# Five adaLN modulations moved to TensorE as 256-column products with the condition stationary

## The chip, the cores and the metric

The kernel runs on one core of a Trainium2 chip. The metric is the device time of one execution in microseconds. The core has five engines with instruction queues of their own: PE (TensorE, with its weight loads shown apart as PEld), DVE (VectorE), ACT (ScalarE), POOL (GpSimd) and SP (SyncE, which here only issues transfers). PE's clock has two levels, 2.4 GHz (1.00 in the profile) and 1.2 GHz (0.50).

## The reference, cut to what matters

Two layers of a hybrid backbone over 128 context and 512 latent tokens, 1024 wide, all in float32. Each layer first makes six modulation vectors from a condition, one set for the context tokens and one for the latent ones:

```
mod = silu(cond) @ w_ada[l] + b_ada[l]          # (1024) @ (1024, 6144), for cond = c_ctx and c
shift1, scale1, gate1, shift2, scale2, gate2 = split(mod, 6)
h = rmsnorm(x, norm1_g) * (1 + scale1) + shift1
x = x + gate1 * mixing(h)                        # latent attention, differential attention, SSD scan, one projection
h = rmsnorm(x, norm2_g) * (1 + scale2) + shift2
x = x + gate2 * (relu(h @ w_ff1)**2 @ w_ff2)
```

Below, a modulation is named (l, j): layer l, and j from 0 to 5 in the order above. One modulation is 1024 x 1024 weights, 4 MB, times two condition vectors.

## The kernel before, in words

Activations lie with features on the 128 partitions and the 640 tokens along the row. Each layer has a mixing part (`mixing`, L571) and a feed-forward part (`feed_forward`, L1845). Large products are done as three products of float32 values split into a high and a low part. The mixing part has five stages: the convolution inputs and values; the remaining projections woven with the SSD scan (`ps_proj`, `ps_ssd`); the scan's tail, woven with the start of differential attention (attention B); attention B with the first part of the output projection (`woc`); latent attention (attention A) with a second part of the output projection. A tail adds the last part of the projection (`wo2`), the residual and the squares and scales for norm2 (`nrm2.scaled`, `nrm2.square`).

The modulations are made as fill work between these. Each is needed late: gate1 (j = 2) where the output projection first adds to x (L539), and shift2 and scale2 (j = 3, 4) where norm2 scales x (L493, L494). There are three ways in which one is made:

- `AdaPE` (L355): at the very start, (0, 1) and (0, 0). Not touched by the change.
- `ada_pe(l, j)` (L439): TensorE with the weights stationary. For each 128 output columns, eight products of a 128 x 128 block of w_ada with the two condition columns (L456), accumulated in one PSUM bank, then a small copy by ACT (L457). A full float32 product stands in the profile as two records, so a step of eight products is 16. Before the change it makes (0, 2) and (0, 3), in 16 steps.
- `ada_rows(items)` (L397): DVE with transposed weights. First PE spreads each condition vector over all partitions (`crow`, L406). Then DVE multiplies each 128 x 512 piece of weights with it and sums along the row (output `junk`, L427). A modulation is 32 such instructions. Before the change it makes (0, 4) in the mixing part of layer 0, (1, 3) and (1, 4) in that of layer 1, and five more in the feed-forward parts, which the change leaves alone.

`ada_first` chains the first layer's three. `gates_made` tells when gate1 of layer 0 is there: after the scan's tail the kernel steps the fill until it is.

The order of the work is written as generators. `weave` (L186) always steps the part with the smallest (k + 0.5) / n, where k counts its steps and n is its pace. The fill's pace is set three times per mixing part by `FILL[l]`: for the projections, for the scan's tail together with attention B, and for attention A; `pace(n)` sets k back to 0. What is left runs behind attention A. The framework places instructions on the engines in an order that starts from this one, and an instruction waits for what it reads and for a free buffer of its kind. Buffers are of a few kinds: G (48 of them, 642 columns), X (6, 648 columns), Y (13, 512 columns), and PSUM banks (PB: 3). All weights and all x tiles are fetched by SP in one queue (wr by L266 and L1745, x by L239).

Of the kernel before, what the change touches and what calls it, by code (L numbers as in the profile page):

```python
# [21 lines left out]
P = 128  # L22
D = 1024
KD = D // P
# [72 lines left out]
SLOT = 576  # L97
GW = T + 2

ADA_T = [(0, 4), (0, 5)] + [(1, j) for j in (1, 0, 2, 3, 4, 5)]  # L100
NG, NX, NXS = 48, 6, 13
NWR, NWH, NWL = 7, 6, 5

# [1 line left out]
def build(nc, tc, a, ctx):  # L105
    vec, act, pool, pe = nc.vector, nc.scalar, nc.gpsimd, nc.tensor
# [7 lines left out]
    def mark(s):  # L114
        if MARK:
            MARK(nc, s)
# [15 lines left out]
    def nm(s):  # L132
        uid[0] += 1
        return f"{s}_{uid[0]}"

    def size(shape):
        n = 1
        for s in shape[1:]:
            n *= s
        return n  # L140
# [11 lines left out]
    def Y(shape, dt=F32, name="t"):  # L152

        assert size(shape) <= 512, shape
        return sp.tile(list(shape), dt, tag="Y", name=nm(name), bufs=NXS)

    def S(shape, tag, bufs=2, dt=F32):
        return sp.tile(list(shape), dt, tag=tag, name=nm(tag), bufs=bufs)
# [4 lines left out]
    def PB(name="pb"):  # L163
        return psp.tile([P, 512], F32, tag="pb", name=nm(name), bufs=3)
# [4 lines left out]
    def f(ap):  # L169
        return ap.bitcast(F32)  # L170
# [52 lines left out]
    ident, ones = f(identr), f(masksr[:, 4])  # L223
# [4 lines left out]
    sc = cp.tile([P, KD, 2], F32, name="sc")  # L228
# [17 lines left out]
    def V(l, name, i=0, n=1):  # L246
        o = VEC[name][0] + i
        return vecs[:, l, o:o + n]
# [56 lines left out]
    def evac_split(hi, lo, src):  # L305
        act.copy(out=hi, in_=src)
        vec.tensor_tensor(out=lo, in0=src, in1=f(hi), op=ALU.subtract)  # L307
# [27 lines left out]
    def ada_finish(l, j, ps, ms=slice(0, KD)):  # L335

        n = ms.stop - ms.start
        b = V(l, "bada", j * 8 + ms.start, n)
        vec.tensor_tensor(out=mods[l][:, j, ms], in0=ps, in1=b.unsqueeze(2).to_broadcast([P, n, 2]), op=ALU.add)
        if j in (1, 4):  # L340
            g = V(l, "g1" if j == 1 else "g2", ms.start, n)
            vec.scalar_tensor_tensor(out=amul[l][:, j // 4, ms], in0=mods[l][:, j, ms], scalar=1.0,
                                     in1=g.unsqueeze(2).to_broadcast([P, n, 2]), op0=ALU.add, op1=ALU.mult)
        if j in (0, 3):
            evac_split(shh[l][:, j // 3, ms], shl[l][:, j // 3, ms], mods[l][:, j, ms])
# [51 lines left out]
    def ada_rows(items):  # L397

        mark("fill")
        row = [[Y([P, 512], name="crow") for _ in range(2)] for _ in range(2)]  # L400
        for v in range(2):
            for h in range(2):
                pt = PB("crow")
                for i in range(4):
                    k = 4 * h + i
                    pe.matmul(pt[:, i * P:(i + 1) * P], sc[:, k, v:v + 1].to_broadcast([P, P]), ident, start=True, stop=True)  # L406
                act.copy(out=row[v][h], in_=pt)
        units = [(l, j, m, h) for l, j in items for m in range(KD) for h in range(2)]

        def fetch(i):  # L410
            l, j, m, h = units[i]
            raw = Y([P, 512], name="wa")
            nc.sync.dma_start(raw, a["w_adaT"][ADA_T.index((l, j)), m, :, h * 512:(h + 1) * 512])
            return raw

        raws = [fetch(0), fetch(1)]
        for i, (l, j, m, h) in enumerate(units):
            if m == 0 and h == 0:
                res = S([P, 2, KD, 2], "adares", 2)
            for v in range(2):  # L420
                junk = X([P, 512], name="junk")
                sum_ = res[:, h, m, v:v + 1]
                if 2 * h + v in ROWS_POOL:
                    pool.tensor_tensor(out=junk, in0=raws[i], in1=row[v][h], op=ALU.mult)
                    act.activation(out=junk, in_=junk, func=AF.Copy, accum_out=sum_)
                else:
                    vec.scalar_tensor_tensor(out=junk, in0=raws[i], scalar=1.0, in1=row[v][h], op0=ALU.mult, op1=ALU.mult,  # L427
                                             accum_out=sum_)
            if i + 2 < len(units):
                raws.append(fetch(i + 2))  # L430
            if h == 1:
                if m == KD - 1:
                    sm = S([P, 8, 2], "adapt", 2)
                    vec.tensor_tensor(out=sm, in0=res[:, 0], in1=res[:, 1], op=ALU.add)
                    ada_finish(l, j, sm)
                yield
                mark("fill")

    def ada_pe(l, j):  # L439

        def fetch(m):
            raw = [Y([P, 4, P], name="wa") for _ in range(2)]
            for h in range(2):
                c = j * 1024 + m * P
                nc.sync.dma_start(raw[h], a["w_ada"][h * 512:(h + 1) * 512, c:c + P].rearrange("(k p) c -> p k c", p=P))
            return raw

        raws = [fetch(0)]
        res = S([P, KD, 2], "adapt", 2)
        for m in range(KD):  # L450
            mark("fill")
            if m + 1 < KD:
                raws.append(fetch(m + 1))
            ps = PB("adap")
            for k in range(KD):
                pe.matmul(ps[:, 0:2], raws[m][k // 4][:, k % 4], sc[:, k], start=(k == 0), stop=(k == KD - 1))  # L456
            act.copy(out=res[:, m], in_=ps[:, 0:2])  # L457
            if m == KD - 1:
                ada_finish(l, j, res)
            yield  # L460

    gates_made = []

    def ada_first():

        for m, _ in enumerate(ada_pe(0, 2)):
            if m == KD - 1:
                gates_made.append(0)
            yield
        yield from ada_pe(0, 3)  # L470
        yield from ada_rows([(0, 4)])

# [96 lines left out]
    def mixing(l, nrm, fill, late=None, raws={}):  # L571
# [1074 lines left out]

        fills = FILL[l]
        pace(fills[0])
# [45 lines left out]
    AHEAD = 1  # L1694
    FETCHED, AHEADS = 7, 2
    AP1, AP0 = (1, 4), ()
    FILL = (2, 20, 9), (8, .01, 9)
    ROWS_POOL = ()
    CONV_POOL = ()
    ON_POOL = {f"xbc{j}" for j in range(2, 6)} | {"dv0", "dv1"}  # L1700
# [299 lines left out]
        act.copy(out=masksr[:, 0:4, :], in_=mk)  # L2000
        act.activation(out=never, in_=mk[:, M_SF:M_SB + 1], func=AF.Copy, scale=-1e30)
    for l in range(DEPTH):
        f0 = Part(ada_first() if l == 0 else ada_rows([(1, 3), (1, 4)]), 1)
        n2 = mixing(l, nrm, f0, *((second, raws0) if l == 0 else ()))
        f1 = Part(ada_rows([(0, 5), (1, 1), (1, 0), (1, 2)] if l == 0 else [(1, 5)]), 57)
        nrm = feed_forward(l, n2, f1)
# [64 lines left out]
def host_inputs(i):  # L2071
    c_ = np.ascontiguousarray
    fm = lambda v: v.reshape(DEPTH, -1, P).transpose(0, 2, 1)
    arr = {}
    x = np.concatenate([i["x_prompt"][0], i["x_sample"][0]], axis=0)
    arr["xT"] = c_(x.reshape(T, KD, P).transpose(2, 1, 0))
    cc = np.stack([i["c_ctx"], i["c"][0]], axis=0)
    arr["cT"] = c_(cc.reshape(2, KD, P).transpose(2, 1, 0))
    ad = i["w_ada"].reshape(DEPTH, D, 6, KD, P)
    arr["w_ada"] = c_(i["w_ada"][0, :, :5 * D])  # L2080
    arr["w_adaT"] = c_(np.stack([ad[l, :, j].transpose(1, 2, 0) for l, j in ADA_T]))
    arr["W"] = _pack(i["w_in"], i["w_uq"], i["w_ukv"], i["w_out"], i["w_ff1"], i["w_ff2"])
    cw = i["ssm_conv_w"].reshape(DEPTH, CONV_K, 6, P).transpose(0, 3, 2, 1).reshape(DEPTH, P, 30)
    gsub = np.concatenate([i["diff_subln_g"]] * 2, axis=1)[:, :, None]
    arr["vecs"] = c_(np.concatenate([fm(i["norm1_g"]), fm(i["norm2_g"]), fm(i["b_ada"]), fm(i["mla_q_norm_g"]),
                                     fm(i["mla_kv_norm_g"]), cw, fm(i["ssm_conv_b"]), gsub, fm(i["ssm_norm_g"])], axis=2))
    row = np.concatenate([i["mla_qk_norm_q"], i["mla_qk_norm_k"], i["diff_q_norm_g"], i["diff_k_norm_g"],
                          i["diff_lq1"], i["diff_lk1"], i["diff_lq2"], i["diff_lk2"],
                          i["ssm_A_log"].reshape(DEPTH, 16), i["ssm_dt_bias"].reshape(DEPTH, 16), i["ssm_D"]], axis=1)
    arr["rows"] = c_(np.broadcast_to(row[:, None, :], (DEPTH, P, NROW)))  # L2090
    arr["cdk"] = c_(i["cache_diff_k"][0].reshape(DEPTH, P, 256))
    arr["cdv"] = c_(i["cache_diff_v"][0].reshape(DEPTH, P, 256))
    arr["ckr"] = c_(i["cache_mla_krope"][0])
    arr["cckvT"] = c_(i["cache_mla_ckv"][0].transpose(0, 2, 1))
    st = i["state_ssm"][0].reshape(DEPTH, 2, 2, 4, P_C, N_C)
    arr["h0"] = c_(st.transpose(0, 2, 5, 1, 3, 4).reshape(DEPTH, P, 512))
    arr.update(_shape_consts())
    return arr
# [31 lines left out]
```

## Time and profile before

| | us |
|---|---|
| three runs: median (lowest to highest) | 1838.31 (1832.51 to 1839.88) |
| the profiled execution | 1843.01 |
| its span, first to last instruction | 1841.2 |
| mean granted clock of PE | 0.948 |
| busy: PE, PEld, DVE, ACT, POOL | 1752.6, 1659.3, 1330.3, 828.8, 464.5 |

The profiled execution is one run with the profiler on; its span leaves out 1.8 us around the instructions. Busy time is the union of an engine's instructions. Matmuls are pipelined, so a record lasts longer than the step from its start to the start of the next; the step is what it costs PE in a run of such records.

### The profile page before, as it was taken

The page shows a single profiled execution, that of the slowest core. Times are in us where ns is not written, and L with a number is a line of the kernel's source. Part 1 is how long each engine was busy: PE and PEld are TensorE (multiplying, and loading weights), DVE is VectorE, ACT ScalarE, POOL GpSimd, SP SyncE. Part 2 cuts the span into 40 slices and gives each one's busy share as a digit, 9 for nine tenths or more (in the row PEclk, how much of TensorE's full clock was granted, in tenths as well). Part 3 has the DMA queues.
Part 4 walks back from the last instruction along what each step waited for, and adds up shares of the span by engine and source line. Part 5 has one row for each costly group of instructions (what it writes and reads, how often), then busy time and mean ns, then how long its engine had stood idle before and what let it go on. Part 6 is the DMA issues. An engine that isn't in the chain of part 4 may idle for free. (4 is left out here: it accounts for less than half of the span.)

```text
span 1841.2 us, 31851 instructions
## 1 busy us (share of the span) xinstructions
PE 1752.6 (95%) x11764; PEld 1659.3 (90%) x11764; DVE 1330.3 (72%) x2788; ACT 828.8 (45%) x1737; POOL 464.5 (25%) x538
## 2 busy tenths in 40 slices
PE   6999999999989999999997999889999999999999
PEld 4798778998989999999997987779999999999998
DVE  6774867568578988685776778989677877475562
ACT  7553327554445452432544443387534445243340
POOL 1433433101120231404135244431003032130400
PEclk8899866899999999999999999889999999999999
DMA  9122113344143437264441232202424242525341
GB/s 336 56 78 71 52 35 88 103 136 146 32 136 117 138 100 260 93 213 154 149 159 48 76 107 68 69 25 84 138 88 127 86 131 81 186 87 161 112 157 56
DMA packets 122732, 209.02 MB, mean 114 GB/s; under 512 B 13392, under 2 KB 32720, under 8 KB 122576
## 3 DMA queue, kind: packets, MB, share of 16 engines
q1 hardware_dynamic: 122016, 206.80, 35.2%
q8 instruction: 93, 1.52, 0.3%
q14 instruction: 63, 0.52, 0.1%
q10 hardware_dynamic: 560, 0.18, 0.0%
HBM read 179.51 MB, written 27.43 MB: 112 GB/s over the span
## 5 line engine op out<-in xcount | busy, mean ns | idle before, releaser
L1775 ACT CAST wh<-wr 128x512 fp32r<-128x512 f32 x232 | 143.9, 621 | 316.0 <-PE fm L1805 205.2
L1805 PE MATMUL fm<-ul,wh 128*128 128x320 f32 x1024 | 235.0, 311 | 10.2 <-DVE ul L307 10.2
L1776 DVE TENSOR_TENSOR wl<-wr,wh 128x512 fp32r<-128x512 f32 x232 | 179.0, 780 | 79.8 <-issue 44.6
L1805 PE MATMUL fm<-uh,wh 128*128 128x320 f32 x1024 | 234.8, 310 | 0.1
L1805 PE MATMUL fm<-uh,wl 128*128 128x320 f32 x1024 | 234.5, 310 | 0.0
L1762 POOL TENSOR_TENSOR wS<-wr,wr 128x512 f32<-128x512 f32 x48 | 78.7, 1639 | 495.2 <-DMA wr<-in_W 213.9
L1805 PEld LDWEIGHTS fm<-ul,wh 128*128 128x128 f32 x1024 | 172.3, 189 | 11.3 <-DVE ul L307 11.3
L427 DVE SCALAR_TENSOR_TENSOR junk<-wa,crow 128x512 f32<-128x512 f32 x256 | 176.7, 739 | 7.4 <-DMA wa<-in_w_adaT 5.7
L1805 PEld LDWEIGHTS fm<-uh,wh 128*128 128x128 f32 x1024 | 172.4, 189 | 0.5 <-issue 0.3
L1805 PEld LDWEIGHTS fm<-uh,wl 128*128 128x128 f32 x1024 | 172.3, 189 | 0.0
L539 DVE SCALAR_TENSOR_TENSOR x<-fm,mod,x 128x128 f32<-128x128 f32 (+2 forms) x192 | 72.5, 432 | 107.7 <-PE fm L1805 104.7
L759 PE MATMUL tm<-wl,hhi 128*128 128x256 f32 (+2 forms) x400 | 120.0, 300 | 5.7 <-POOL wl L297 4.0
L1775 ACT CAST wh<-wS 128x512 fp32r<-128x512 f32 x96 | 59.8, 622 | 141.7 <-PE fm L1805 70.5
L758 PE MATMUL tm<-wh,hhi 128*128 128x256 f32 (+2 forms) x400 | 120.0, 300 | 3.0 <-DVE zth L779 2.4
L760 PE MATMUL tm<-wh,hlo 128*128 128x256 f32 (+2 forms) x400 | 119.2, 298 | 0.0
L296 ACT CAST wh<-wr 128x512 fp32r<-128x512 f32 (+2 forms) x108 | 66.8, 625 | 75.6 <-PE fm L318 34.6
L1805 PE MATMUL ffx<-eh,wh 128*128 128x320 f32 x288 | 89.4, 311 | 0.0
L1805 PE MATMUL ffx<-eh,wl 128*128 128x320 f32 x288 | 88.9, 309 | 0.0
L1805 PE MATMUL ffx<-el,wh 128*128 128x320 f32 x288 | 88.9, 309 | 0.0
L759 PEld LDWEIGHTS tm<-wl,hhi 128*128 128x128 f32 x400 | 80.2, 200 | 8.0 <-POOL wl L297 4.2
L539 DVE SCALAR_TENSOR_TENSOR x<-wo,mod,x 128x128 f32<-128x128 f32 (+1 forms) x144 | 57.0, 432 | 39.0 <-PE wo L318 38.5
L758 PEld LDWEIGHTS tm<-wh,hhi 128*128 128x128 f32 x400 | 80.1, 200 | 5.1 <-DVE zth L779 2.8
(386 smaller groups left out, 4837.1 us busy)
## 6 DMA issues: line engine op xcount, KB each, us to landing
wr<-in_W SPq DMA_DIRECT2D x351, 256.0 KB, 2.8
wa<-in_w_adaT SPq DMA_DIRECT2D x128, 256.0 KB, 4.5
xsave<-x SPq DMA_DIRECT2D x72, 320.0 KB, 2.2
x<-xsave SPq DMA_DIRECT2D x72, 320.0 KB, 4.0
war<-in_w_ada SPq DMA_DIRECT2D x32, 256.0 KB, 5.3
wa<-in_w_ada SPq DMA_DIRECT2D x32, 256.0 KB, 3.4
x<-in_xT SPq DMA_DIRECT2D x16, 320.0 KB, 5.5
out_yT<-x SPq DMA_DIRECT2D x8, 320.0 KB, 2.2
```

The costliest lines, as they stand in the source:

```text
L296: act.copy(out=hi[:, :w], in_=raw[:, :w])
L427: vec.scalar_tensor_tensor(out=junk, in0=raws[i], scalar=1.0, in1=row[v][h], op0=ALU.mult, op1=ALU.mult, accum_out=sum_)
L539: vec.scalar_tensor_tensor(out=x[m][:, t0:t0 + n], in0=src, scalar=mods[l][:, j, m, v:v + 1], in1=x[m][:, t0:t0 + n], op0=ALU.mult, op1=AL ...
L758: pe.matmul(ps[:, i, :n], hh[k][:, ts], hi[:, c:c + n], start=s, stop=False)
L759: pe.matmul(ps[:, i, :n], hh[k][:, ts], lo[:, c:c + n], start=False, stop=False)
L760: pe.matmul(ps[:, i, :n], hl[k][:, ts], hi[:, c:c + n], start=False, stop=e)
L1762: pool.tensor_tensor(out=box[key], in0=box[x0], in1=box[x1], op=op)
L1775: act.copy(out=hi, in_=raw)
L1776: vec.tensor_tensor(out=lo, in0=raw, in1=f(hi), op=ALU.subtract)
L1805: mm = pe.matmul(o, w_, x_[:, ts], start=s_, stop=e_, skip_group_check=on)
```

## The change

One function takes the place of `ada_pe` and `ada_first`, and of `ada_rows` in the mixing parts. `ada_stream` makes the five modulations (0, 2), (0, 3), (0, 4), (1, 3), (1, 4). The two condition columns are stationary, the weights stream as they are. A unit is a quarter of a modulation: four transfers of 256 KB (pieces of 1 KB) into four G buffers, fetched a unit ahead; eight products of 256 columns in a row; a copy of the two rows by ACT into an X buffer; and one step later two transposes and `ada_finish` for the quarter. There are 12 units in layer 0 and 8 in layer 1. `ada_rows` in the feed-forward parts stays. The paces are set anew.

```diff
-ADA_T = [(0, 4), (0, 5)] + [(1, j) for j in (1, 0, 2, 3, 4, 5)]
+ADA_S = [(0, 2), (0, 3), (0, 4), (1, 3), (1, 4)]
+ADA_T = [(0, 5)] + [(1, j) for j in (1, 0, 2, 5)]
...
-    def ada_pe(l, j):
...
+    def ada_stream(items):
+
+        units = [(l, j, qr) for l, j in items for qr in range(4)]
+
+        def fetch(i):
+            l, j, qr = units[i]
+            c = (ADA_S.index((l, j)) * 4 + qr) * 256
+            raw = [G([P, 2, 256], name="ws") for _ in range(4)]
+            for h in range(4):
+                nc.sync.dma_start(raw[h], a["w_adaS"][h * 256:(h + 1) * 256, c:c + 256].rearrange("(k p) c -> p k c", p=P))
+            return raw
+
+        def finish(i, row):
+            l, j, qr = units[i]
+            pt = PB("adat")
+            for m in range(2):
+                pe.transpose(pt[:, 2 * m:2 * m + 2], row[:2, m * P:(m + 1) * P], ident[:2, :2])
+            ada_finish(l, j, pt[:, :4].rearrange("p (m v) -> p m v", v=2), slice(2 * qr, 2 * qr + 2))
+            if j == 2 and qr == 3:
+                gates_made.append(l)
+
+        raws, row = [fetch(0)], None
+        for i, u in enumerate(units):
             mark("fill")
+            if i + 1 < len(units):
+                raws.append(fetch(i + 1))
             ps = PB("adap")
             for k in range(KD):
-                pe.matmul(ps[:, 0:2], raws[m][k // 4][:, k % 4], sc[:, k], start=(k == 0), stop=(k == KD - 1))
+                pe.matmul(ps[:2, :256], sc[:, k], raws[i][k // 2][:, k % 2], start=(k == 0), stop=(k == KD - 1))
+            if row is not None:
+                finish(i - 1, row)
+            row = X([P, 256], name="adarow")
+            act.copy(out=row[:2], in_=ps[:2, :256])
             yield
+        mark("fill")
+        finish(len(units) - 1, row)
+        yield
...
-    def ada_first():
...
-    FILL = (2, 20, 9), (8, .01, 9)
+    FILL = (1.5, 9, 8), (.51, 4, 8)
...
-        f0 = Part(ada_first() if l == 0 else ada_rows([(1, 3), (1, 4)]), 1)
+        f0 = Part(ada_stream(ADA_S[:3] if l == 0 else ADA_S[3:]), 1)
...
+    arr["w_adaS"] = c_(np.concatenate([ad[l, :, j].reshape(D, D) for l, j in ADA_S], axis=1))
```

## Rows read from the trace of the kernel before

**Rows 1.** The page: share of the span by engine; granted clock in 40 slices.
```profile
PE 1752.6 (95%) x11764; PEld 1659.3 (90%) x11764; DVE 1330.3 (72%) x2788; ACT 828.8 (45%) x1737; POOL 464.5 (25%) x538
...
PEclk8899866899999999999999999889999999999999
```

**Rows 2.** Windows by stage: length, busy PE, PEld, DVE, ACT, POOL; clock, DMA, GB/s.
```profile
175.00:268.00 93.00, 90.43 (x479) 72.79 (x479) 63.41 (x117) 28.91 (x71) 37.59 (x32) 0.80 0.14 41
268.00:305.00 37.00, 33.09 (x137) 27.79 (x133) 24.85 (x72) 23.09 (x61) 13.58 (x29) 0.50 0.33 91
305.00:403.00 98.00, 97.40 (x698) 90.33 (x697) 67.50 (x192) 58.24 (x145) 18.39 (x39) 0.89 0.35 106
403.00:493.00 90.00, 85.64 (x696) 83.52 (x695) 55.38 (x144) 41.11 (x92) 5.14 (x7) 0.98 0.31 102
493.00:528.00 35.00, 28.40 (x178) 27.32 (x178) 31.07 (x58) 18.25 (x34) 16.89 (x19) 0.95 0.19 54
985.00:1100.00 115.00, 109.45 (x748) 100.97 (x749) 87.55 (x178) 52.04 (x116) 46.22 (x68) 0.96 0.26 79
1100.00:1177.00 77.00, 72.87 (x472) 59.92 (x473) 68.38 (x132) 28.81 (x70) 34.57 (x24) 1.00 0.22 67
1177.00:1216.00 39.00, 27.48 (x107) 20.86 (x104) 33.28 (x96) 23.92 (x62) 19.41 (x39) 0.57 0.11 34
1216.00:1286.00 70.00, 68.67 (x515) 62.68 (x513) 61.80 (x178) 52.83 (x125) 16.68 (x34) 1.00 0.22 71
1286.00:1365.00 79.00, 77.93 (x654) 76.83 (x653) 52.95 (x133) 38.97 (x90) 4.09 (x3) 1.00 0.38 125
1365.00:1407.00 42.00, 35.45 (x205) 33.62 (x203) 36.97 (x83) 18.87 (x34) 15.63 (x23) 0.88 0.17 48
```

**Rows 3.** The same windows for the tile adap alone: PE, PEld, ACT; their sum.
```profile
268.00:305.00 37.00, 10.44 (x48) 10.96 (x48) 0.47 (x3) 0.50 0.33 91
305.00:403.00 98.00, 21.24 (x176) 21.36 (x176) 1.62 (x11) 0.89 0.35 106
...
sum 890.00, PE 35.36 PEld 36.08 ACT 2.55; mean PE 2.95 PEld 3.01 ACT 0.21
```

**Rows 4.** Groups (busy, mean ns): crow, junk; then layer 1's windows of junk on DVE.
```profile
L406 PE MATMUL crow<-identr,sc 128*128 128x128 f32 x128 | 15.9, 276 | 0.0
L427 DVE SCALAR_TENSOR_TENSOR junk<-wa,crow 128x512 f32<-128x512 f32 x256 | 176.7, 739 | 7.4 <-DMA wa<-in_w_adaT 5.7
...
1100.00:1177.00 77.00, 14.04 (x25) 1.00 0.22 67
...
1365.00:1407.00 42.00, 5.88 (x20) 0.88 0.17 48
sum 422.00, DVE 48.56; mean DVE 8.09
```

**Rows 5.** Timeline of PE (start, length): 384-column float32 products; four small transposes.
```profile
349.50 1.45 PE L1340 MATMUL qa<-wuq,cqf 128*128 128x384 f32 x4
...
58.74 0.41 PE L390 MATMUL adat<-identr,adarow 4*128 4x4 f32 x4 [0.67 <-ACT adarow L388]
```

**Rows 6.** Timeline of PE at a two-column group; the window behind it, as rows 2.
```profile
243.47 1.84 PE L456 MATMUL adap<-sc,wa 128*128 128x2 f32 x16
245.17 1.08 PE L1164 MATMUL yd<-xtm,eg 128*128 128x64 f32 x8
...
248.00:268.00 20.00, 20.00 (x63) 15.55 (x65) 11.89 (x19) 5.30 (x11) 7.27 (x11) 0.50 0.14 40
```

**Rows 7.** Waits of SP and PE (us, times, longest); transfers (KB, us to landing).
```profile
SPq L239 <- PE yT L1250: 42.8, 2, 31.1
...
PE kva L1303 <- DMA wukv<-in_W: 2.1, 2, 1.2
...
wa<-in_w_ada SPq DMA_DIRECT2D x32, 256.0 KB, 3.4
```

More of the change, by code (lines that the diff above doesn't have):

```diff
@@ L437, in ada_rows @@
                 mark("fill")
-    def ada_pe(l, j):
[L441 to L445, printed above, removed]
-            return raw
-        raws = [fetch(0)]
-        res = S([P, KD, 2], "adapt", 2)
-        for m in range(KD):
+    def ada_stream(items):
[6 more added lines that the diff above has]
+                nc.sync.dma_start(raw[h], a["w_adaS"][h * 256:(h + 1) * 256, c:c + 256].rearrange("(k p) c -> p k c", p=P))
+            return raw
+        def finish(i, row):
[8 more added lines that the diff above has]
+        for i, u in enumerate(units):
@@ L451, in ada_pe @@
             mark("fill")
-            if m + 1 < KD:
-                raws.append(fetch(m + 1))
+            if i + 1 < len(units):
+                raws.append(fetch(i + 1))
             ps = PB("adap")
             for k in range(KD):
-                pe.matmul(ps[:, 0:2], raws[m][k // 4][:, k % 4], sc[:, k], start=(k == 0), stop=(k == KD - 1))
-            act.copy(out=res[:, m], in_=ps[:, 0:2])
-            if m == KD - 1:
-                ada_finish(l, j, res)
+                pe.matmul(ps[:2, :256], sc[:, k], raws[i][k // 2][:, k % 2], start=(k == 0), stop=(k == KD - 1))
@@ L460, in ada_pe @@
+            if row is not None:
+                finish(i - 1, row)
+            row = X([P, 256], name="adarow")
+            act.copy(out=row[:2], in_=ps[:2, :256])
             yield
+        mark("fill")
+        finish(len(units) - 1, row)
+        yield
     gates_made = []
-    def ada_first():
[L466 to L471, printed above, removed]
```

## The prediction

> **What bounds the kernel now.** I read the page first: PE is busy 95% of the span, DVE 72%, and the line of granted clocks shows that PE is not always at its upper level [rows 1]. A busy PE at half its clock is time that could come back, so the next view is the table of windows, cut at the stages of the two mixing parts, the only places that the change touches [rows 2]. The first six rows are layer 0, the other five layer 1. In each row compare PE's busy time with the length, then DVE's, then the clock.
>
> What is to be seen: in the projections (175 to 268 and 1100 to 1177), the output projection with attention B (305 to 403, 1216 to 1286) and attention A (403 to 493, 1286 to 1365) PE is busy for all but 1 to 5 us of each stretch. There, work added to PE is paid in full. Between (268 to 305, 1177 to 1216) PE idles 4 and 11.5 us and its clock is 0.50 and 0.57: chains over several engines set the pace. In the tail (493 to 528, 1365 to 1407) DVE is the busier engine beside PE, and layer 1 takes 42 us where layer 0 takes 35. The other thing is the clock [rows 2]: the projections of layer 0 have 0.80, those of layer 1 have 1.00, though they run the same instructions. Layer 0 has the two-column products besides.
>
> **What goes, what comes.** The prediction is summed against the profiled execution (1843.0 us, span 1841.2), and since that lies 4.7 us above the median of the runs, 1838.3, the same difference is then taken from the median.
>
> PE loses the two modulations of layer 0 whose weights are stationary: 256 records, 35.4 us in sum, of which 10.4 lie in 268 to 305 and 21.2 in 305 to 403 [rows 3]. It also loses the spreading of the condition for the row products, twice 32 of the 128 crow records: 15.9/4, or 4.0 us per layer [rows 4].
>
> PE gains 20 units (12 in layer 0, 8 in layer 1) of eight full float32 products with 256 streaming columns. No such product with two stationary columns stands in the trace, but the stationary side loads beside the stream, and one with 384 columns does stand there: four records take 1.45 us, the last one's own 0.49 taken off leaves 0.32 for each step, which is 0.84 ns per column [rows 5]. So 256 columns cost 0.215 us, a product is two records, a unit 16: 3.4 us at the upper clock, twice that at the lower. The two transposes of a unit are four records, as the 0.41 us of the adat row [rows 5]. A unit is 3.85 us then: 46 us in layer 0, 31 in layer 1. Net on PE: 46 - 35.4 - 4.0 = +6.6 in layer 0, 31 - 4.0 = +27 in layer 1, **+33 in all**, if nothing else changed.
>
> The Trainium skill (TensorE: Matmul & The Clock Gate, Back-to-back issue gap) has N / 2.4 + 2.5 ns as the warm gap of an isolated matmul. By that a record of 256 columns would take 109 ns, an estimate from that page, and the 320 records 34 us less; the 384-column row does not agree (an estimate of 162 ns by the page, 320 measured), since these are float32 records. So the row's price stands in the sum.
>
> DVE loses 96 of the 256 products with junk as output, 0.69 us each [rows 4]: 22 us in layer 0 (in its attention A), 48.6 us in layer 1. It gains some 40 additions on two columns each in place of the few on 16, and ACT gains 20 copies of two rows against 16 small and 8 wide ones that go; both have idle time in every stretch, and I cost them at nothing. If that cover were gone, 20 copies at about 0.3 us would be 6 us.
>
> SP issues 80 transfers of 256 KB before and after: 16 for each modulation. Four now wait for buffers of the wide kind (G) rather than of kind Y, in one queue with the wr weights. That queue has waited 31.1 us at one point for one G buffer [rows 7], so G looks short just there; I cost it at 0 here (the fetch is a unit ahead, and landing takes 3.4 us [rows 7]), and at 12 us as the upper end: three fresh starts of about 4 us each, a landing and an issue.
>
> **Where the units fall.** The pace is (k + 0.5) / n. In layer 0, n = 1.5 lets one unit into the projections (the second would be due at 1.0), n = 9 some three into 268 to 305 and six into 305 to 403, and two are left for attention A. In layer 1, 0.51 makes the first due at 0.98, past the last step of the projections; then one in 1177 to 1216, three to 1286, four in attention A.
>
> **The sum, layer 0.** Projections: two groups of 16 records (3.7 us) for one unit (3.85): 0. But the clock: a 16-record group at 243.47 and eight 64-column products run without a gap, and the clock then is 0.50 from 248 to 268, with PE fully busy [rows 6]. The loss in 175 to 268 is 93 x (1 - 0.80) = 18.6 us [rows 2], and layer 1 shows 1.00 without those groups. Bounds 0 and -18.6; I take -12, nearer to the layer 1 row, because PE's 2.6 idle us in this stretch may cost clock as before. 268 to 305: three units, 11.5 us at the upper level and 22 at the lower, for 10.4: from -4 (PE idle, warmer clock) to +11, taken as +3. 305 to 403: six units, 23.1, for 21.2, +2; the clock's loss is 98 x 0.11 = 10.8 us, and I take half, -5. Attention A: two units, +7.7, less 4.0 for crow, less 2 of the 4.4 us that PE idles there while DVE's row products run: +2. Layer 0: 0 - 12 + 3 + 2 - 5 + 2 = **-10**.
>
> **The sum, layer 1.** To 1177: crow -4.0; PE idles 5.5 + 4.1 us, and DVE, 68.4 of 77 us busy in the second stretch, loses 14 there: -4. From 1177 to 1216: DVE's row products stand in front of the scan's tail; PE has 11.5 us free, into which one unit fits: bounds +4 and -8, taken -3. To 1286: three units, +11.5. Attention A: four units, +15.4, less 1. Tail: the last row products (5.9 us on DVE [rows 4]) run ahead of the last residuals and of the scale that norm2 waits for; without them it is like layer 0's 35 us: -6 of 7. Layer 1: -4 - 4 - 3 + 11.5 + 14.4 - 6 = **+9**.
>
> Together -1, so 1842 for the profiled execution and **1837** against the median: no change that can be told (a measurement of this kernel tells about 0.5%, 9 us).
>
> **Rivals.**
> *The clock comes back wholly (faster).* The 18.6 and 10.8 us of layer 0 return but for 3, and units that stream 256 columns keep PE warm in 268 to 305 as well. For it: two stretches with the same instructions, 0.80 and 1.00. Against: falls in 1177 to 1216 come without any such group. Then -26 in place of -17, -4 in place of +3, and 3 more from DVE in layer 1: 1838.3 - 1 - 19 = 1818. Chance 0.24.
>
> *The clock does not come back (slower).* What lowers it are the other short products (64 columns, one column) and idle moments, which stay; the units then run in part at the lower level. For it: the clock also falls where no group is near. Then the -17 is 0, and 268 to 305 gives +8: 1838.3 - 1 + 22 = 1859. It decides from the point where the clock of 175 to 268 stays under 0.85. The Trainium skill says on the same page (What's actually happening) that the clock returns to the half rate after an idle window; by that rule, a stretch without a gap before 248 should not have lost its clock, and the groups would be blameless. The trace disagrees at 246 to 268, where PE is busy throughout. Chance 0.22.
>
> *A new wait.* A transfer for a unit waits for a G buffer, weights queue behind it on SP, and PE, in order, stands at the unit: +12, so 1849. For it the 31.1 us; against it, PE's one wait for a DMA in the mixing parts took 1.2 us at most [rows 7]. Chance 0.09.
>
> *The unit is cheaper than the row.* Two stationary columns let a record stream at half the price: 320 x 0.107 = 34 us less, 1803. Nothing in the trace shows it. Chance 0.02.
>
> **How the numbers follow.** The forecast has 0.43; its own range is 1825 to 1848, from the bounds of the terms. Of it 0.07 lies below 1829, 0.03 above 1847.5. Faster by over 0.5%: 0.24 + 0.02 + 0.07 = 0.33. Slower: 0.22 + 0.05 (the new wait, over half) + 0.03 = 0.30. Same: 0.37. The range to hold 8 in 10 reaches from the fast rival's better half to the slow rival: 1812 to 1861.
>
> **What would show it.** Right: adap records of 256 columns, some 320, spaced 0.215 us at the upper level; clock of the stretch that was 175 to 268 over 0.9; attention A of layer 1 longer by 10 to 16 us with PE full; the tail of layer 1 near 35 us. Wrong: PE waiting for DMA ahead of adap, the scan's tail longer than now, or a clock near 0.8 in layer 0's projections.

## The result and the profile after

| | before | after |
|---|---|---|
| median, us (lowest to highest) | 1839.1 (1832.51 to 1849.32, 4 runs) | 1862.95 (1856.82 to 1869.29, 4 runs) |
| ratio after / before, 95% interval | | 1.0111 [1.0079, 1.0144] |
| the profiled execution; its span | 1843.01; 1841.2 | 1856.82; 1855.0 |
| mean granted clock of PE | 0.948 | 0.971 |

The change makes the kernel slower by 1.1%, some 20 us by the ratio (24 by the medians); no change that can be told was forecast. The time lies 2 us above the range. The profiled execution of after is the shortest of its four, so the two traces differ by 13.8 us only. The mean granted clock goes with that: the four executions took 1869.29, 1864.64, 1861.27 and 1856.82 us at 0.965, 0.968, 0.969 and 0.971. So the trace shows after at its highest clock, 6 us under its median; where a reading hangs on that, it is said.

The page of after, the lines that answer to [rows 1]:

```profile
PE 1766.1 (95%) x11804; PEld 1623.8 (88%) x11804; DVE 1274.5 (69%) x2620; ACT 828.8 (45%) x1739; POOL 459.3 (25%) x538
...
PEclk7999989999999999999998999799999999999999
```

PE is busy for 13.5 us more, although its clock is higher, and DVE for 56 us less. The busiest engine got the work, and an engine with idle time was relieved.

The windows by stage of after, columns as in [rows 2]; the first five are layer 0 (so are the first five of [rows 2], where the prediction counts six):

```profile
160.80:251.70 90.90, 89.81 (x571) 73.51 (x569) 64.79 (x128) 30.44 (x73) 36.30 (x29) 0.96 0.19 56
251.70:280.20 28.50, 21.89 (x105) 13.98 (x105) 22.37 (x65) 20.61 (x54) 13.86 (x29) 0.82 0.33 100
280.20:379.30 99.10, 93.76 (x612) 72.72 (x613) 69.95 (x201) 59.38 (x144) 19.18 (x44) 0.97 0.33 103
379.30:480.10 100.80, 100.25 (x758) 86.49 (x756) 39.60 (x92) 41.73 (x97) 4.82 (x7) 1.00 0.30 98
480.10:512.50 32.40, 27.20 (x170) 26.11 (x171) 30.98 (x57) 18.21 (x34) 16.30 (x18) 0.95 0.18 52
1076.50:1161.70 85.20, 85.20 (x548) 71.67 (x545) 62.83 (x122) 30.34 (x73) 30.40 (x25) 0.98 0.14 39
1161.70:1200.60 38.90, 28.68 (x111) 19.23 (x112) 29.02 (x77) 23.36 (x61) 18.46 (x38) 0.65 0.28 87
1200.60:1284.90 84.30, 80.58 (x573) 68.48 (x572) 65.52 (x196) 57.08 (x138) 16.73 (x34) 1.00 0.27 84
1284.90:1383.40 98.50, 97.89 (x743) 84.32 (x741) 38.00 (x86) 39.96 (x92) 4.84 (x7) 1.00 0.31 100
1383.40:1417.70 34.30, 27.65 (x174) 26.57 (x174) 31.06 (x57) 18.30 (x34) 16.27 (x18) 0.95 0.19 54
```

Three things are to be seen. The clock of layer 0's projections is 0.96 where it was 0.80. PE is full in both attentions A (100.25 of 100.8, 97.89 of 98.5), and these are the longest. And the scan's tail of layer 1, 1161.7 to 1200.6, still idles 10 us at a clock of 0.65, with a unit in it.

For a comparison both traces are cut at the same products: the first `cums`, the last `tm`, the first `wo`, the first `scA`, the last `oT`, the first `nss`. Lengths in us, and the forecast of the change beside them:

| stage | layer 0 before, after | change | forecast | layer 1 before, after | change | forecast |
|---|---|---|---|---|---|---|
| projections (`cums` to last `tm`) | 140.2, 126.0 | -14.2 | -12 | 125.3, 123.1 | -2.2 | -8 |
| scan's tail (to `wo`) | 38.1, 28.5 | -9.6 | +3 | 34.8, 39.0 | +4.2 | -3 |
| attention B (to `scA`) | 97.2, 99.1 | +1.9 | -3 | 75.7, 84.4 | +8.7 | +11.5 |
| attention A (to last `oT`) | 90.2, 100.8 | +10.6 | +2 | 79.2, 98.4 | +19.2 | +14.4 |
| tail (to `nss`) | 32.9, 31.3 | -1.6 | 0 | 40.0, 33.1 | -6.9 | -6 |
| all five | | -12.9 | -10 | | +23.0 | +9 |

The rest of the 13.8 us: the feed-forward part and the end behind layer 1's mixing are 2.8 us longer, all that lies around layer 0's mixing 1 us. The 2.8 us are work that changed sides: between the last `oT` and the first `nss` of layer 1 stand 73 records of the feed-forward part (`fm`) in before and 54 in after, and the windows from there to the end have 2908 and 2928 records of PE:

```profile
1405.50:1841.20 435.70, 427.65 (x2908) 426.84 (x2906) 273.35 (x476) 162.97 (x298) 73.52 (x49) 1.00 0.39 122
1416.50:1855.00 438.50, 430.41 (x2928) 429.56 (x2926) 273.60 (x477) 163.07 (x299) 74.63 (x49) 0.99 0.38 121
```

So layer 1's tail and what follows it belong together: -6.9 + 2.8 = -4.1 us.

A unit of after, first by its groups (tile `adap` and its copy: lowest, median and highest ns, first and last start), then in the timeline of PE, then the windows of attention B of layer 1 and of both attentions A for `adap` alone:

```profile
L468 PEld LDWEIGHTS adap<-ws,sc x320: 80/85/129, 174.8 to 1368.6; 128*2 128x2 f32 x160
L468 PE MATMUL adap<-ws,sc x320: 377/379/631, 174.8 to 1368.8; 128*2 128x256 f32 x160
...
L472 ACT COPY adarow<-adap x20: 346/362/363, 178.4 to 1369.2; 2x256 f32<-2x256 f32 x20
```
```profile
1309.41 3.62 PE L468 MATMUL adap<-ws,sc 128*2 128x256 f32 x16
1312.95 0.28 PE L456 MATMUL adat<-identr,adarow 2*128 2x2 f32 x2
1313.16 0.44 PE L1398 MATMUL pT<-identr,prob 128*128 128x128 f32 x2
```
```profile
1200.60:1284.90 84.30, 7.23 (x32) 2.55 (x32) 0.72 (x2) 1.00 0.27 84
1284.90:1383.40 98.50, 18.23 (x80) 6.29 (x80) 1.81 (x5) 1.00 0.31 100
379.30:480.10 100.80, 18.07 (x80) 6.38 (x80) 1.81 (x5) 1.00 0.30 98
```

There are 320 records, as forecast. In the unit at 1309.41 the last record's own 0.379 us off 3.62 leaves 3.24 for 15 steps, 0.216 us each; 0.215 was taken from [rows 5]. Its transposes are two records, not the four of the forecast, and from its start to that of the next work, at 1313.16, the unit takes 3.75 us. Each attention A holds 80 records, five units. The forecast had two and four there; by stage the units of layer 0 stand 1, 1, 5 and 5 (forecast 1, 3, 6 and 2), those of layer 1 0, 1, 2 and 5 (forecast 0, 1, 3 and 4).

The waits of after, by the queue of SP and by PE (in all, times, longest):

```profile
SPq L449 <- PE scBc L1536: 28.2, 2, 20.7
SPq L449 <- PE adap L468: 20.6, 9, 13.2
```
```profile
PE kva L1310 <- DMA wukv<-in_W: 1.1, 1, 1.1
```

The new transfers (L449) do wait for buffers, 20.7 us once. But PE waits for a DMA no longer than before [rows 7].

### The profile page after: what moved, and what is told of

Read it like the earlier page. It is cut to its first block, busy times and chain, and to the rows that moved or that the text cites. A ratio compares the mean times of both kernels' runs of the same rounds, so it can differ in the third digit from the quotient of the medians.

```text
span 1855.0 us, 31726 instructions
## 1 busy us (share of the span) xinstructions
PE 1766.1 (95%) x11804; PEld 1623.8 (88%) x11804; DVE 1274.5 (69%) x2620; ACT 828.8 (45%) x1739; POOL 459.3 (25%) x538
## 3 DMA queue, kind: packets, MB, share of 16 engines
q1 hardware_dynamic: 119968, 206.80, 34.8%
## 5 line engine op out<-in xcount | busy, mean ns | idle before, releaser
L1812 PE MATMUL fm<-ul,wh 128*128 128x320 f32 x1024 | 235.3, 311 | 10.2 <-DVE ul L308 10.2
L428 DVE SCALAR_TENSOR_TENSOR junk<-wa,crow 128x512 f32<-128x512 f32 x160 | 106.5, 718 | 0.7 <-DMA wa<-in_w_adaT 0.7
```

The lines of the kernel that those rows point to most:

```text
L1812: mm = pe.matmul(o, w_, x_[:, ts], start=s_, stop=e_, skip_group_check=on)
```

## The experiments

Each kernel was timed in turns with the kernel before; a ratio is to before's runs on the same chip.

**Layer 0 alone, and layer 1 alone.** The first keeps the row products in layer 1, the second keeps all of layer 0 as before.

```diff
-ADA_S = [(0, 2), (0, 3), (0, 4), (1, 3), (1, 4)]
+ADA_S = [(0, 2), (0, 3), (0, 4)]
...
-    FILL = (1.5, 9, 8), (.51, 4, 8)
+    FILL = (1.5, 9, 8), (8, .01, 9)
...
-        f0 = Part(ada_stream(ADA_S[:3] if l == 0 else ADA_S[3:]), 1)
+        f0 = Part(ada_stream(ADA_S) if l == 0 else ada_rows([(1, 3), (1, 4)]), 1)
```

> The change in layer 0 alone; layer 1 makes its two modulations by row products on VectorE as before, with the old paces. Theory (the layers add up: layer 0 gains its clock back, layer 1 pays its units in full on TensorE): the profiles of before and after give layer 0 as 14.6 us shorter up to its second norm, so 1839 - 15 = 1824 us, 1817 to 1831, with a granted clock near 1.00 in the projections of layer 0. Rival (the clock of layer 0 came back in the profiled execution only, the median runs of the change lie 6 us above it): 1835 to 1842, same as before.

```diff
...
-    FILL = (2, 20, 9), (8, .01, 9)
+    FILL = (2, 20, 9), (.51, 4, 8)
...
-        f0 = Part(ada_first() if l == 0 else ada_rows([(1, 3), (1, 4)]), 1)
+        f0 = Part(ada_first() if l == 0 else ada_stream(ADA_S), 1)
```

> The change in layer 1 alone; layer 0 as before with its two-column groups and row products. Theory (the layers add up): the profiles give layer 1 as 23.8 us longer, so 1839 + 24 = 1863 us, 1857 to 1870. Rival (part of the loss of layer 1 comes from what layer 0 leaves behind, buffers or an order of work that shifts): 1848 to 1855.

Layer 0 alone: 1838.25 us (10 runs), ratio 0.9986 [0.9967, 1.0006], or -2.6 us against 1844.15: not the 15 us expected, and within the rival's range. Layer 1 alone: 1866.53, ratio 1.0137 [1.0101, 1.0173], or +25 us, as expected. Within the noise the two add up to the whole change. So layer 1 sets the result, and layer 0 gives less than its 10 us. One reason stands in the first window of its trace (layer 0 alone, projections):

```profile
162.60:258.60 96.00, 95.73 (x571) 77.66 (x569) 64.95 (x128) 30.43 (x73) 35.78 (x29) 0.89 0.18 53
```

The instructions are those of after in the same stretch (571 records of PE in both), but the clock is 0.89 and not 0.96, and the stretch is 5 us longer. The trace is 2.6 us shorter than that of before, like the runs, and shows where the rest went: layer 0's mixing is 7.2 us shorter, the stretch between the two mixing parts 2.9 longer, layer 1's mixing 1.6 longer. Against the rival's reason, a clock that came back in the profiled execution only, stand the mean clocks: 0.960 to 0.969 in the ten executions, 0.947 to 0.954 in those of before on this chip.

**The row products of layer 1 left out.** The kernel before, with constants in the place of (1, 3) and (1, 4). It shows what those products cost when nothing replaces them.

```diff
+    vec.memset(mods[1][:, 3:5], 0.0)
+    vec.memset(amul[1][:, 1], 1.0)
+    evac_split(shh[1][:, 1], shl[1][:, 1], mods[1][:, 3])
...
-        f0 = Part(ada_first() if l == 0 else ada_rows([(1, 3), (1, 4)]), 1)
+        f0 = Part(ada_first() if l == 0 else iter(()), 1)
```

> The kernel before with the modulations (1, 3) and (1, 4) left out: constants stand in their place, and no row products run in the mixing part of layer 1. It tells what taking them off VectorE can give at most. Theory (TensorE was hardly held up by them: the spreading of the condition, 3.6 us, and the tail, 7 us, are all): 1839 - 10 = 1829 us, 1825 to 1832. Rival (VectorE also held up the projections and the tail of the scan, as the prediction took it): 1839 - 21 = 1818 us, 1812 to 1822.

1836.97 us, ratio 0.9952 [0.9931, 0.9973]: 9 us (5 to 13), about the 10 expected, not the 22 us which the prediction's relief terms (18) and its hidden unit (4) come to. The profiled execution is the shortest of ten, 1825.05 us. Its windows of the second half of the projections, the scan's tail and the tail of layer 1:

```profile
1080.40:1165.50 85.10, 85.10 (x547) 71.34 (x545) 65.28 (x122) 30.28 (x72) 31.11 (x25) 0.98 0.14 39
1165.50:1196.50 31.00, 21.25 (x94) 16.86 (x94) 25.74 (x72) 20.85 (x54) 18.22 (x34) 0.67 0.14 42
1352.90:1384.60 31.70, 26.61 (x162) 25.57 (x163) 30.32 (x56) 17.71 (x34) 16.23 (x18) 0.95 0.19 51
```

PE's idle time in the projections is gone, yet the stretch from the first `cqss` takes 85.1 us, against 84.8 in before. Its clock is 0.98 where before has 1.00; with row products and a clock of 0.98, in the trace of layer 0 alone, the stretch takes 85.9 us. So they held it up by some 1 us, not by the 4 that PE idles there. The scan's tail is 3.7 us shorter and the last tail 8.3, of which some 3 come back behind it. And the scan's tail still idles 9.8 us: these were not DVE's row products. From here to layer 1 alone is 30 us by the medians, 34 by the ratios: 3.7 to 4.3 us for each of eight units, against 3.85 in the forecast. On the whole none is hidden.

**One product of eight.** The kernel after, with seven eighths of every modulation's sum left out: all transfers, copies and transposes stay.

```diff
-            for k in range(KD):
-                pe.matmul(ps[:2, :256], sc[:, k], raws[i][k // 2][:, k % 2], start=(k == 0), stop=(k == KD - 1))
+            for k in range(1):
+                pe.matmul(ps[:2, :256], sc[:, k], raws[i][k // 2][:, k % 2], start=(k == 0), stop=(k == 0))
```

> The changed kernel with one product in each unit in place of eight (7/8 of the sums of the five modulations are left out); transfers, copies and transposes stay. Theory (a unit is paid in full on TensorE): 20 units x 14 records x 0.222 us = 62 us less than the changed kernel, 1863 - 62 = 1801 us, 1796 to 1810. Rival (units lie partly in time that TensorE has free, or they hold its clock up): 25 to 45 us less, 1818 to 1838.

1805.83 us, ratio 0.9803 [0.9773, 0.9833]: 57 us less than after's 1862.95, for 280 records less (320 to 40), or 0.204 us each. That is 94% of the 0.216 us step. So the products cost nearly their full price on the path that sets the end, as expected. What transfers, copies and transposes cost doesn't show here, since they stay; the 3.7 to 4.3 us for a unit above, of which the 16 records are 3.5, leave them some 0.2 to 0.8 us, within the noise. The group in its trace:

```profile
L468 PE MATMUL adap<-ws,sc x40: 377/378/634, 176.1 to 1314.7; 128*2 128x256 f32 x40
```

**No two-column group in layer 0's projections.** The kernel before with one pace changed, to test the clock by itself.

```diff
-    FILL = (2, 20, 9), (8, .01, 9)
+    FILL = (.01, 20, 9), (8, .01, 9)
```

> The kernel before with the first pace of layer 0 at 0.01 in place of 2: the two groups of two-column products leave the projections of layer 0 and run later, all else is as before. Theory (those groups are what takes the clock of the projections down): the clock between the column sums and the end of the projections is 0.95 or more, these 92 us shrink by 3.7 for the groups and by 8 to 15 for the clock, 3.7 come back later: 1844 - 11 = 1833 us, 1828 to 1837. Rival (other short products or idle moments take it down): the clock there stays near 0.80, 1842 to 1846.

1842.98 us, ratio 1.0000 [0.9979, 1.0022]. Its windows of layer 0, the second half of the projections to attention A:

```profile
162.50:249.10 86.60, 86.60 (x548) 72.39 (x546) 63.41 (x122) 30.37 (x73) 30.76 (x25) 0.96 0.14 39
249.10:289.00 39.90, 30.36 (x142) 25.37 (x142) 28.07 (x75) 22.15 (x58) 20.15 (x38) 0.61 0.37 104
289.00:388.90 99.90, 98.99 (x683) 91.58 (x684) 67.06 (x194) 60.85 (x148) 18.59 (x39) 0.87 0.34 102
388.90:487.90 99.00, 92.90 (x745) 90.66 (x744) 56.13 (x146) 41.79 (x95) 5.71 (x7) 0.97 0.33 106
```

The clock of the projections is 0.96 with the groups gone, and these take 121.6 us, not 140.2: -18.6, of which 3.7 are the groups' own. But the groups run later, and what comes later is longer: the scan's tail by 1.9 us, attention B by 2.6, attention A by 8.8. In the trace 7 us are left of layer 0, in the runs nothing: of the theory the clock came true, not the time. The mean clock of the ten executions is 0.953, that of before's on this chip 0.951 (medians). The clock returned in this stretch; over the whole execution it hardly rose.

One pair of traces could be chance, so here is the clock of the same stretch (first `cqss` to last `tm`) in all twelve kernels. In layer 0 with the two groups it is 0.79, 0.80, 0.80 and 0.85, without them 0.89 to 0.98 in eight. So the groups, or the order of work that comes with them, do lower it. PE's idle time isn't needed for that: layer 0 of the kernel without row products in layer 1 has the groups and PE busy throughout, in the first line. But the 1.00 of layer 1 was that execution's: the other ten traces without groups have 0.87 to 0.98. The second line is layer 1 of the kernel with the early pace, further below, which runs the same instructions as before up to there and takes 10 us more.

```profile
173.30:262.70 89.40, 89.40 (x478) 72.93 (x476) 62.67 (x116) 28.59 (x70) 37.70 (x32) 0.79 0.15 43
```
```profile
1091.10:1185.90 94.80, 90.91 (x544) 75.92 (x542) 74.02 (x156) 29.39 (x71) 30.66 (x24) 0.87 0.20 61
```

**Two-column groups put into layer 1.** The kernel after with two such groups (results unused) in layer 1's projections, the opposite test.

```diff
+    def with_groups():
+        groups = ada_pe(0, 2)
+        for _ in range(2):
+            next(groups)
+            yield
+        yield from ada_stream(ADA_S[3:])
...
-    FILL = (1.5, 9, 8), (.51, 4, 8)
+    FILL = (1.5, 9, 8), (2, 4, 8)
...
-        f0 = Part(ada_stream(ADA_S[:3] if l == 0 else ADA_S[3:]), 1)
+        f0 = Part(ada_stream(ADA_S[:3]) if l == 0 else with_groups(), 1)
```

> The changed kernel with two groups of sixteen two-column records put into the projections of layer 1 (their results go nowhere). Theory (the groups take the clock down): the stretch from the column sums to the end of the projections in layer 1 has a clock of 0.75 to 0.90 where it had 0.96 to 1.00, and the time is that of the change plus 3.7 for the groups and 5 to 15: 1863 + 14 = 1877 us, 1870 to 1882. Rival (it takes something that only layer 0 has): clock as it was, 1865 to 1868.

1867.52 us, ratio 1.0133 [1.0092, 1.0175], 4.6 us above after's median: the rival's time, not the 14 us expected. The two groups in the timeline of PE, and the windows behind them:

```profile
1089.81 1.84 PE L495 MATMUL adap<-sc,wa 128*128 128x2 f32 x16
...
1160.84 1.84 PE L495 MATMUL adap<-sc,wa 128*128 128x2 f32 x16
```
```profile
1097.70:1107.90 10.20, 10.20 (x31) 6.66 (x31) 4.99 (x13) 4.63 (x10) 4.01 (x4) 0.50 0.03 8
1161.00:1175.00 14.00, 14.00 (x87) 11.33 (x86) 10.93 (x16) 3.87 (x8) 7.77 (x10) 1.00 0.05 10
```

Behind the first group, 6 us later and after a run of 30 one-column `cqss` products, the clock is 0.50 for 10 us, though PE is busy throughout; behind the second it stays at 1.00. The fall isn't the group's alone: after, without a group, is at 0.50 there from 1085.8 to 1089.2, behind the same `cqss` products, and layer 0 of the kernel with layer 0 alone, with no group near, for 10.3 us from 169.0. From the first `cqss` to the last `tm` the clock is 0.94, expected were 0.75 to 0.90; the stretches of layer 1 without groups have 0.87 to 1.00. So here no loss by the groups can be told. Most of the 4.6 us is the groups' own 3.7.

**Layer 0 streams two modulations only.** (0, 2) and (0, 3) by units, (0, 4) and layer 1 by rows; then the same with one pace, so that layer 1's last row products run earlier.

```diff
-ADA_S = [(0, 2), (0, 3), (0, 4), (1, 3), (1, 4)]
+ADA_S = [(0, 2), (0, 3)]
...
+    def first_fill():
+        yield from ada_stream(ADA_S)
+        yield from ada_rows([(0, 4)])
...
-    FILL = (1.5, 9, 8), (.51, 4, 8)
+    FILL = (1.5, 9, 9), (8, .01, 9)
...
-        f0 = Part(ada_stream(ADA_S[:3] if l == 0 else ADA_S[3:]), 1)
+        f0 = Part(first_fill() if l == 0 else ada_rows([(1, 3), (1, 4)]), 1)
```

> The change for (0, 2) and (0, 3) alone; (0, 4), (1, 3) and (1, 4) by row products as before. Theory (each streamed unit is paid in full where TensorE is full, row products are not): against the change in layer 0 alone (1838, ratio 0.9986) four units leave, 4 x 3.85 us, and the spreading comes back, 3.4 us, with 3 to 4 us of idle TensorE: 1838 - 8 = 1830 us, ratio 0.992 to 0.996. Rival (the row products of (0, 4) hold up attention A about as much as the units do): ratio 0.997 to 1.000.

```diff
-    FILL = (1.5, 9, 9), (8, .01, 9)
+    FILL = (1.5, 9, 9), (8, .01, 14)
```

> The kernel before this one in the list with the pace of layer 1's attention A at 14 in place of 9, so that the last row products end some 25 us ahead of the tail. Theory (the last row products on VectorE hold up the tail of layer 1, 41 us where without them it is 34): 6 us less than with pace 9, ratio 0.989 to 0.993. Rival (the same products in front of the softmax of attention A cost there what they save in the tail): no difference from pace 9, within 2 us.

1835.24 us, ratio 0.9954 [0.9929, 0.9979]; and 1829.08, ratio 0.9926 [0.9903, 0.9948], which beats both kernels; both came as expected. Streaming (0, 4) too, as layer 0 alone does, thus costs some 6 us over rows (-2.6 against -8.5, on two chips; the intervals allow 0 to 12).

**That pace alone.** The kernel before with it.

```diff
-    FILL = (2, 20, 9), (8, .01, 9)
+    FILL = (2, 20, 9), (8, .01, 14)
```

> The kernel before with one pace changed: the fill of layer 1's attention A has 14 in place of 9, so that its last row products end within attention A and not in the tail. Theory: the tail term of the prediction is the whole of what the kernel with early rows gained over its twin without: the tail (last oT to first nss) is 34 in place of 40 us, attention A the same length, the time 6 us (0.3%) under before. Rival: the 6 us come only along with layer 0's part of that kernel, or attention A takes back what the tail gains: the time of before.

1839.68 us, ratio 0.9986 [0.9969, 1.0004]: -2.6 us (-6 to +1), with -6 expected. Its trace can't decide by its length: the execution is the longest of twelve, with layer 1's projections at 0.87, as shown above. The window of layer 1's tail with the late rows, with the early rows, and in this kernel:

```profile
1353.20:1393.60 40.40, 32.77 (x188) 30.59 (x188) 36.35 (x80) 18.83 (x34) 15.40 (x22) 0.92 0.17 46
```
```profile
1359.90:1393.80 33.90, 28.95 (x188) 27.76 (x188) 29.70 (x58) 18.83 (x34) 15.62 (x18) 1.00 0.20 55
```
```profile
1375.30:1410.80 35.50, 30.26 (x189) 29.09 (x189) 31.27 (x58) 18.99 (x34) 14.91 (x18) 0.95 0.19 53
```

DVE has 22 instructions fewer in the tail, and it is 4.5 to 6.5 us shorter than with the late rows (40.0 in before). In the timed runs the step between the twins was 5.2 us by the ratios, here 2.6; both agree with some 4, but by itself the 2.6 is not clear of noise.

**No unit in the scan's tail.** The kernel after with other paces in layer 1.

```diff
-    FILL = (1.5, 9, 8), (.51, 4, 8)
+    FILL = (1.5, 9, 8), (.51, 1.2, 10)
```

> The kernel after with other paces in layer 1: no unit in the scan's tail, one in attention B, seven in attention A. Theory: the unit in the scan's tail stands in PE's queue ahead of products that the tail's chain waits for and runs at the lower clock, so it cost some 7.5 us there and costs 3.7 elsewhere: the tail (last tm to first wo) goes back from 39.0 to about 31.5, attention B is some 3.5 us shorter, attention A some 7.5 longer, and the whole is 4 us (0.2%) faster than after. Rival (the unit costs the same wherever it stands): the time is that of after, and what the tail gets back attention A and B lose in full. Rival (the unit filled idle time in the tail, as the prediction had it): 3.5 us slower than after.

1861.46 us, ratio 1.0108 [1.0088, 1.0127]: after's time. What the unit does in after's tail, in the timeline of PE:

```profile
1192.95 1.86 PE L468 MATMUL adap<-ws,sc 128*2 128x256 f32 x4
...
1196.45 3.72 PE L468 MATMUL adap<-ws,sc 128*2 128x256 f32 x12
1200.10 1.13 PE L1310 MATMUL kva<-wukv,cqf 128*128 128x512 f32 x2
1200.66 0.71 PE L319 MATMUL wo<-mCh,wh 128*128 128x320 f32 x1
```

And without it, the windows of layer 1's last four stages, then `adap` alone in them:

```profile
1161.10:1192.70 31.60, 22.39 (x95) 17.22 (x95) 26.39 (x74) 21.04 (x55) 17.97 (x37) 0.66 0.14 40
1192.70:1275.00 82.30, 79.93 (x545) 68.83 (x544) 66.29 (x193) 57.82 (x137) 17.68 (x36) 0.92 0.28 87
1275.00:1382.20 107.20, 105.65 (x781) 88.98 (x782) 40.76 (x94) 42.63 (x99) 4.74 (x7) 1.00 0.35 114
1382.20:1418.70 36.50, 30.51 (x173) 26.94 (x172) 29.98 (x56) 18.02 (x34) 15.48 (x18) 0.91 0.16 44
```
```profile
1192.70:1275.00 82.30, 3.94 (x16) 1.11 (x16) 0.36 (x1) 0.92 0.28 87
1275.00:1382.20 107.20, 21.89 (x97) 7.61 (x98) 2.17 (x6) 1.00 0.35 114
1382.20:1418.70 36.50, 3.57 (x16) 1.23 (x16) 0.36 (x1) 0.91 0.16 44
```

The tail is 7.4 us shorter (39.0 to 31.6), as expected: in after the unit's records came there for the most part at the lower clock, and the last twelve ran straight ahead of `kva` and the first `wo`. But attention B gave back 2.2 us only, for one unit less. Its clock is 0.92 where after has 1.00, since it stays at 0.50 until 1205.2, 12.5 us into that stage, while in after it had risen within the tail, at 1198.5, while the unit ran; by 82.3 x 0.08 that is some 6.6 us, an estimate. Attention A took 8.9 more, with one unit more, and the last tail 3.3, since a unit now runs there. In all +2.6 in the trace and -1.5 in the runs. The rival that a unit costs the same wherever it stands comes closest, but the -4 of the theory and the +3.5 of the other rival lie within the noise of the two ratios. That the last tail would hold a unit was not foreseen, so this run doesn't price the tail's place alone.

## Why the prediction was wrong, point by point

- **The price of a unit was right.** 0.216 us for a step against 0.215, 3.75 us for a unit with its transposes against 3.85. The rule of the Trainium skill (TensorE: Matmul & The Clock Gate, Back-to-back issue gap), weighed against the row and set aside, would have made it 109 ns, an estimate from that page; the trace disagrees, and so does the run with one product of eight (0.204 us for each record that went). The rival of a cheaper unit is out.
- **Layer 1 is where it failed: +9 forecast, +25 measured by layer 1 alone.** The eight units were priced rightly at 31 us; what was to be set against them was summed to 22 us from idle times, and leaving the row products out gave 9. Three steps of the prediction hold the difference. *"PE has 11.5 us free, into which one unit fits"*, taken as -3, came out as +4.2. That idle time lies in a chain over several engines, at a low clock; it is 10 us with the unit there and without it. What stood in front of the chain was worth 3.7 us (row products left out), and the unit took 7 to 8. *The relief of the projections*, -8, came out as -2.2, about the crow records alone. PE's idle time there went, as foreseen, and the stretch did not get shorter: at the same clock the row products held it up by some 1 us (85.9 against 85.1), and 1.7 us went to 3.4 us at the lower clock, which before's execution did not have. *The place of the units*: one fewer in attention B, one more in A, so B and A together cost 27.9 where 25.9 was forecast; that is a shift, no miss of price.
- **The tail term was right in its mechanism, and somewhat too large**: -6 against -6.9 at the cut, but -4.1 with the 2.8 us of products that then run behind it. The kernel without row products in layer 1 has some 3 us there too, and no unit. The pace alone gave 2.6 (-1 to 6) in the runs.
- **Layer 0: -10 forecast, -12.9 in the trace, -2.6 (-6 to +1) in the runs.** The step on the projections' clock, -12, held in the trace: 0.80 to 0.96, as it also does when only the groups leave, and in all twelve traces the stretch has a higher clock without them. The scan's tail was better than its term (-9.6 against +3), because its groups went, one unit stood there for the three of the forecast, and its clock rose to 0.82. Attention A was worse (+10.6 against +2), with five units for two; tail, attention B and attention A together came to +2.9 against +2. What failed is to take one trace for every run: before's trace has a mean clock of 0.948, its nineteen executions beside layer 0 alone a median of 0.951; after's trace has 0.971, its executions 0.9685; and the same 571 records had 0.89 in one trace and 0.96 in another. In the trace of layer 0 alone the mixing gains 7.2 us, and 4.5 are lost behind it. How the clock lies within the timed runs can't be seen, so how much of the rest is clock stays open.
- **The rivals.** The time came out near that of *the clock does not come back* (1859) by chance: by its own test (a clock under 0.85 in layer 0's projections) that rival did not happen. *The clock comes back wholly* did happen there, without its time. *A new wait* did not: SP waits, PE does not. By the rule of the Trainium skill on the same page (What's actually happening), that the clock falls after idle time, the groups would have been blameless. The traces disagree: in layer 0 of the kernel without row products in layer 1 PE is busy for 89.40 of 89.40 us, and the clock is 0.79.

In one sentence: the change moves some 75 us of units to the engine that has hardly any free time, and what it takes off there is 35 us of two-column products and 8 of spreading, and besides work of an engine that held up little.

## What to carry to other kernels

Before work is moved to the busiest engine, run the kernel without that work at all: here the row products were worth 9 us where 22 had been summed from idle times, and 30 us of units replaced them. Idle time of the bound engine inside a chain over several engines is not free room: here a unit of 3.75 us put there ran ahead of the next link and lengthened the stage by 7.4 us, some of which the next stage got back in clock. A gain in the clock is worth what the end of the program shows, not what the stage shows, and one trace's clock is to be held against the clocks of the other executions first.

## What the runs showed of the hardware that was not expected

- The clock falls with PE busy without a gap: 0.79 over 89.4 us without idle time (layer 0, two groups). It falls behind `cqss` products with and without a group near (3.4 us at 0.50 in after, 10.2 with a group), and it didn't fall behind the second group in layer 1 (1.00 for 14 us). Which of the short products it takes isn't shown.
- The same instructions ran at a mean clock of 0.89 in one trace and 0.96 in another, and in layer 1's projections at 0.87 (the kernel with the early pace, 94.8 us) and 1.00 (before, 84.8 us). So one profile doesn't tell the clock of the other executions.
- A product with two stationary columns costs the same for each streaming column as one with 128 (0.216 us for 256, against 0.32 for 384 in [rows 5]): its weight load is 85 ns, against some 190 in the two-column products (128 stationary columns), and the step shows no saving from it.
